# Block 1's attention: projections cut into pieces of six matmuls, one carried along by each step of the heads

## The chip, the core and the metric

One core of a Trainium2 chip runs one program: three transformer blocks in a row over 512 tokens of width 1024, in float32. The metric is the device time of one execution in microseconds (us). The matrix engine is TensorE (PE), with VectorE (DVE), ScalarE (ACT), GpSimd (POOL) beside it, and SyncE (SP), which issues most of the DMAs.

## The reference, cut to what matters

Only the mixer of the first block is touched by the change.

```python
h = rms_norm(x, mix_norm[l])
proj = h @ w_in[l]
qa, ka, va, qb, kb, vb = [proj[..., offs[i]:offs[i + 1]] for i in range(6)]
# 8 heads of two 32-wide halves, each with a relative bias
s1 = einsum(q1, k1) * scale + bias;  s2 = einsum(q2, k2) * scale + bias
p = softmax(s1) - lam * softmax(s2);  oa = p @ va
oa = rms_norm(oa, diff_subln[l]) * (1.0 - lambda_init)
# 8 heads of 64, four to each of two key/value heads
qb = rms_norm(qb, q_norm[l]); kb = rms_norm(kb, k_norm[l])
qb = apply_rope(qb, cos, sin); kb = apply_rope(kb, cos, sin)
ob = softmax(qb @ kb.T * scale) @ vb
x = x + concatenate([oa, ob], axis=-1) @ w_out[l]
```

## The kernel before

Activations lie transposed, as 8 panels of 128 features by 512 tokens. A float32 product is made of three fp32r matmuls, high by high, high by low and low by high (`mm3x`, lines 116 to 122). So a weight panel of 128x1024 goes through four stations: its load on SP's queue (`raw`, line 157), its high part on ACT and its low part on DVE, or on GpSimd where `pool_lo` is set (both in `weight`, lines 137 and 138), and 24 matmuls of 512 columns on PE.

`mix1` has two phases. In "att", `heads1` makes the projections and the heads, and `half_res` adds the first half of the output product (8 panels of 12 matmuls) to the residual. In "wo" the second half follows (line 526).

`heads1` first projects keys and queries: `rope(4)` for the rotated keys of the grouped heads, and for c = 0 and 1 `proj_q`, `proj_k` and `rope(c)`: 7 panels. A projected panel q or k is scaled on DVE (`scaled`, line 595), split into high and low part in a tile `hl` of which there is one (`HL = 1`; `parts`, lines 481 and 482), written to DRAM (line 487), and read back row by row as the operands of a head (`operand`, line 602; `keys`, line 586; `mk_gqa`, line 678). The panels of `rope` are normed over the head, rotated (GpSimd, lines 572 and 573) and take the same way. The values are projected by `v_tokens` with tokens as output rows, in two halves of 320 columns (192 matmuls).

`attend` runs 16 heads, a differential one and a grouped one by turns, in 4 steps of 128 queries, then 4 steps for the last head's values. A step makes the scores of this head (line 615 or 639, banks a and b), their softmax (DVE lines 617, 623, 624, 629, 640; ACT line 473; GpSimd lines 626 and 627 in steps 0 and 2), and one key chunk of the product with the values for the head before it (`values`): 4 transposes (line 450, banks c and d), a copy on ACT (line 458) and a subtraction on DVE (line 459), and two matmuls (lines 460 and 461), or one in plain float32 for the last chunk (line 454). The last matmul of a step is put down in `marks`.

The other projections hang on the heads: at a grouped head with r = 0, `mk_gqa` projects q and k for c + 2, for c = 0 `v_tokens` too, and `mk_diff` with r = 1 makes `rope(c + 2)`; all 24 matmuls of a panel stand in one block of the program, bank h. `half_res` comes after the heads in the program; each of its panels is told to go on PE after a mark of the second half of the heads (`M0`, `M1`), and its low parts are made by GpSimd (`PA`).

The order of the instructions on each engine is not written out: a list scheduler of the compiler takes, by modelled times, what is ready, earlier program text first. `issue_after(i)` adds that what it encloses comes after i on i's engine.

Of the kernel before, what the change touches and what calls it, by code (L numbers as in the profile page):

```python
# [33 lines left out]
class K:  # L34
# [3 lines left out]
    NL = 4  # L38
    AH = 2
    HL = 1  # L40
    PLH = 4
# [3 lines left out]
    PQ = (0, 2)  # L45
    M0 = 4
    M1 = 30
    PA = True
    OWN = 3
# [368 lines left out]

    def attend(self, heads):
# [72 lines left out]

    def v_tokens(self, src, xhl, vt, rtok, nh):

        nc = self.nc
        for half in range(2):
            pv = [self.psum("cdef") for _ in range(4)]
            for k0, kn in ((0, 3), (3, 3), (6, 2)):
                W = self.weight(src[half][:, k0 * 320:(k0 + kn) * 320], kn * 320, kn)
                for q in range(4):  # L500
                    s = slice(q * 128, (q + 1) * 128)
                    self.mm3x(pv[q][:, :320], [(xhl[k0 + k][0][:, s], xhl[k0 + k][1][:, s]) + W[k] for k in range(kn)], k0 == 0, k0 == 6)
            for q in range(4):
                hv = vt[q][:, half * 5:half * 5 + 5]
                pvv = pv[q][:, :320].rearrange("p (h d) -> p h d", h=5)
                nc.scalar.activation(hv[:, :, 0:64], pvv, AF.Copy, scale=rtok[:, q:q + 1])
                nc.vector.scalar_tensor_tensor(out=hv[:, :, 64:128], in0=pvv, scalar=rtok[:, q:q + 1], in1=f32v(hv[:, :, 0:64]), op0=ALU.mult, op1=ALU.subtract)

    def mix1(self, inp, gnext):
        nc, D = self.nc, self.D  # L510
        xhl, (rb, rtok), res = inp
        outer = self.ph
        gs = self.ph.tile([128, 1], F32, name="subln")
        nc.vector.tensor_scalar(out=gs, in0=self.vec("diff_subln"), scalar1=1.0 - (0.8 - 0.6 * math.exp(-0.0)), scalar2=None, op0=ALU.mult)
        gq, ind = self.vec("qk_norm1"), self.vec("ind1")
        ocs = [self.keep("oc", 8) for _ in range(8)]
        with self.phase("att"):
            self.heads1(xhl, rb, rtok, gq, ind, ocs)
            part = self.half_res(ocs, gs, res)
# [14 lines left out]

    def half_res(self, ocs, gs, res):

        nc, D = self.nc, self.D
        ohl = self.o_parts(ocs, gs, (0, 4, 1, 5), "x", 16)
        part = self.dr.tile([8, 128, 512], F32, name="part")
# [9 lines left out]
        return part  # L549

    def heads1(self, xhl, rb, rtok, gq, ind, ocs):
        nc, D = self.nc, self.D
# [3 lines left out]

        def rope(c, name, kind="pj"):

# [3 lines left out]
            f0 = self.t("rf0")  # L562
            nc.vector.tensor_mul(f0, self.proj(D["w1_in"][8 + c], xhl, kind=kind), rb)
            st = self.psum("st")
# [11 lines left out]
            nc.vector.scalar_tensor_tensor(out=f, in0=p, scalar=1.0 if c == 4 else -0.125, in1=rot, op0=ALU.mult, op1=ALU.mult)  # L576
            return self.parts(f, name)

        d = rope(4, "kpd", "mm")

        def keys(kv):
            ds = []
            for i in range(2):
                t = self.keep("kg", 2, F32R)
                for r in range(2):
                    nc.sync.dma_start(out=f32v(t[64 * r:64 * r + 64]), in_=self.part_rows(d, i, 32 * kv, [(64, 2), (1, 32)]))
                ds.append(t)
            return ds


        vt = [self.keep("vt", 4, F32R, w=1280).rearrange("p (h d) -> p h d", h=10) for _ in range(4)]

        def scaled(tag, p, scale):
            f = self.t("af")
            nc.vector.scalar_tensor_tensor(out=f, in0=p, scalar=scale, in1=rb, op0=ALU.mult, op1=ALU.mult)
            return self.parts(f, tag)

        def operand(tag, d, r, order):

            t = self.keep(tag, 3, F32R, tag="op1", w=1024).rearrange("p (r w) -> p r w", r=2)  # L600
            for b, o in enumerate(order):
                nc.sync.dma_start(out=f32v(t[32 * b:32 * b + 32]), in_=self.part_rows(d, o, 64 * r, [(1, 32), (32, 2)]))
            return t

        def diff_head(h, sms, q2, k2):
# [4 lines left out]
            def unit(q):  # L610
                mx = self.small("mx", 2, 4)
                es = []
                for s in range(2):
                    p = self.psum("scores")
                    nc.tensor.matmul(p, q2[:96, s, q * 128:(q + 1) * 128], k2[:96, s], start=True, stop=True)
                    e0 = self.ld("e0") if s == 0 else self.keep("e1", 12)
# [27 lines left out]

        qds, kds, qgd = {}, {}, {}

# [8 lines left out]

        def proj_q(c, kind="pj"):
            qds[c] = scaled("qdd", self.proj(D["w1_in"][c], xhl, kind=kind), -(32 ** -0.5))

        def proj_k(c, kind="pj"):
            kds[c] = scaled("kdd", self.proj(D["w1_in"][4 + c], xhl, kind=kind), 1.0)  # L660

        def mk_diff(c, r):
            if r == 1:
                qgd[c + self.AH] = rope(c + self.AH, "qpd") if c < 4 - self.AH else None
            return diff_head(2 * c + r, sms[c], operand("qd", qds[c], r, (0, 0, 1)), operand("kd", kds[c], r, (0, 1, 0)))

        def mk_gqa(c, r):
            if r == 0:
                if c == 0:
                    self.v_tokens(D["w1_v"], xhl, vt, rtok, 5)  # L670
                if c % 2 == 0:
                    kg[c // 2] = keys(c // 2)
                if c < 4 - self.AH:
                    proj_q(c + self.AH)
                    proj_k(c + self.AH)
            t = self.keep("qg", 2, F32R)
            for i in range(2):
                nc.sync.dma_start(out=f32v(t[64 * i:64 * i + 64]), in_=self.part_rows(qgd[c], i, 32 * r, [(64, 2), (1, 32)]))
            return gqa_head(r, sms[4 + c], t, kg[c // 2])

# [17 lines left out]

        for c in range(self.AH):
            proj_q(c, "mm")  # L700
            proj_k(c, "mm")
            qgd[c] = rope(c, "qpd", "mm")
        heads = []
        for c in range(4):
            for r in range(2):
                h = 2 * c + r
                heads.append((lazy(lambda c=c, r=r: mk_diff(c, r)), [v[:, h] for v in vt], r, ocs[c], normed(c) if r else None))
                heads.append((lazy(lambda c=c, r=r: mk_gqa(c, r)), [v[:, 8 + h // 4] for v in vt], r, ocs[4 + c], normed(4 + c) if r else None))
        self.attend(heads)

# [1260 lines left out]
def layout(I):  # L1971
# [8 lines left out]
    A["w1_in"] = panels(np.concatenate([w[:, :1024], w[:, 1536:2176][:, perm]], 1))  # L1980
    A["w1_v"] = moving(np.concatenate([w[:, 1024:1536], w[:, 2176:]], 1), 320)

# [71 lines left out]
```

## Time and profile before

| | us |
|---|---|
| median of three runs | 2684.18 |
| lowest to highest run | 2683.64 to 2689.05 |
| the profiled execution | 2690.05 |
| its span, from first to last instruction | 2688.2 |

The profile is of one execution, 5.9 us above the median. Its page gives the busy time of each engine over the span; views of the trace give the same for stretches, the chain of work that ended last, single instructions in order of time, and groups of instructions. A busy PE is not a PE at its rate: a matmul's shown duration includes its way through the array, and the next one starts before it ends. The rate is the distance between starts.

### The profile page before, as it was taken

The page shows a single profiled execution, that of the slowest core. Times are in us where ns is not written, and L with a number is a line of the kernel's source. Part 1 is how long each engine was busy: PE and PEld are TensorE (multiplying, and loading weights), DVE is VectorE, ACT ScalarE, POOL GpSimd, SP SyncE. Part 2 cuts the span into 40 slices and gives each one's busy share as a digit, 9 for nine tenths or more (in the row PEclk, how much of TensorE's full clock was granted, in tenths as well). Part 3 has the DMA queues.
Part 4 walks back from the last instruction along what each step waited for, and adds up shares of the span by engine and source line. Part 5 has one row for each costly group of instructions (what it writes and reads, how often), then busy time and mean ns, then how long its engine had stood idle before and what let it go on. Part 6 is the DMA issues. An engine that isn't in the chain of part 4 may idle for free.

```text
span 2688.2 us, 31177 instructions
## 1 busy us (share of the span) xinstructions
PE 2603.7 (97%) x11820; PEld 2104.6 (78%) x11820; DVE 1558.5 (58%) x2416; ACT 1057.1 (39%) x1622; POOL 410.6 (15%) x335
## 2 busy tenths in 40 slices
PE   8999998989999999999999899999899899999999
PEld 7887787767888887988788677888788777878787
DVE  7866555888544544567433654333545977747564
ACT  4222233666422324555323533223433454424242
POOL 1011012232000004133112301001210313101000
PEclk9999999989999999999999899999999999999999
DMA  5565644433522324422224342222524634223223
GB/s 197 179 202 196 202 154 140 141 99 123 193 94 94 94 93 148 133 100 71 94 96 140 110 144 91 97 98 95 179 73 148 208 99 148 100 94 97 94 92 110
DMA packets 114593, 340.00 MB, mean 126 GB/s; under 512 B 13784, under 2 KB 15768, under 8 KB 114314
## 3 DMA queue, kind: packets, MB, share of 16 engines
q1 hardware_dynamic: 104010, 301.02, 34.3%
q0 software_dynamic: 10432, 36.97, 4.4%
q8 instruction: 93, 1.52, 0.2%
q14 instruction: 58, 0.48, 0.1%
HBM read 301.47 MB, written 40.67 MB: 127 GB/s over the span
## 4 chain that ended last, share of the span: by engine, by line
PE 79%; issue 8%; DVE 5%; DMA 4%; ACT 2%; POOL 1%; SPq 0%; POOLq 0%; ACTq 0%; DVEq 0%
PE c L122 4%; PE a L120 4%; PE a L122 4%; PE c L120 4%; PE e L122 4%; PE a L121 4%; PE e L121 4%; PE c L121 4%; PE e L120 4%; PE b L122 4%; PE b L120 4%; PE b L121 4%; PE f L120 4%; PE d L120 4%; PE d L121 4%
## 5 line engine op out<-in xcount | busy, mean ns | idle before, releaser
L137 ACT ACTIVATE whi<-wraw 128x1024 fp32r<-128x1024 f32 (+5 forms) x422 | 426.0, 1012 | 1037.0 <-PE a L121 180.0
L138 DVE TENSOR_TENSOR wlo<-wraw,whi 128x1024 fp32r<-128x1024 f32 (+5 forms) x410 | 494.3, 1208 | 349.7 <-ACT whi L137 327.1
L120 PE MATMUL e<-xh,whi 128*128 128x512 f32 x368 | 145.1, 394 | 1.6 <-ACT xh L884 1.6
L121 PE MATMUL e<-xl,whi 128*128 128x512 f32 x368 | 145.8, 396 | 0.4 <-DVE xl L885 0.4
L122 PE MATMUL e<-xh,wlo 128*128 128x512 f32 x368 | 144.9, 394 | 0.8 <-DVE wlo L138 0.8
L121 PE MATMUL a<-xl,whi 128*128 128x512 f32 x352 | 139.0, 395 | 4.6 <-DVE xl L182 4.6
L120 PE MATMUL a<-xh,whi 128*128 128x512 f32 x352 | 139.5, 396 | 0.5 <-ACT whi L137 0.5
L122 PE MATMUL a<-xh,wlo 128*128 128x512 f32 x352 | 138.7, 394 | 0.9 <-DVE wlo L138 0.9
L120 PE MATMUL c<-xh,whi 128*128 128x512 f32 x352 | 138.7, 394 | 0.0
L121 PE MATMUL c<-xl,whi 128*128 128x512 f32 x352 | 138.7, 394 | 0.0
L122 PE MATMUL c<-xh,wlo 128*128 128x512 f32 x352 | 138.2, 393 | 0.0
L120 PE MATMUL b<-xh,whi 128*128 128x512 f32 x304 | 120.9, 398 | 10.1 <-ACT xh L181 7.6
L122 PE MATMUL b<-xh,wlo 128*128 128x512 f32 x304 | 120.4, 396 | 1.8 <-DVE wlo L138 1.8
L178 ACT ACTIVATE hh<-h 128x512 fp32r<-128x512 f32 x98 | 61.8, 631 | 148.5 <-DVE h L357 92.6
L121 PE MATMUL b<-xl,whi 128*128 128x512 f32 x304 | 120.2, 395 | 0.0
L896 POOL TENSOR_TENSOR acc<-sq 128x512 f32<-128x512 f32 x11 | 15.4, 1397 | 666.7 <-ACT sq L284 401.4
L122 PE MATMUL f<-xh,wlo 128*128 128x512 f32 x280 | 109.4, 391 | 0.6 <-DVE wlo L138 0.6
L120 PE MATMUL f<-xh,whi 128*128 128x512 f32 x280 | 109.8, 392 | 0.0
L121 PE MATMUL f<-xl,whi 128*128 128x512 f32 x280 | 109.5, 391 | 0.0
L122 PE MATMUL d<-xh,wlo 128*128 128x512 f32 x272 | 106.5, 392 | 0.0
L121 PE MATMUL d<-xl,whi 128*128 128x512 f32 x272 | 106.4, 391 | 0.0
L120 PE MATMUL d<-xh,whi 128*128 128x512 f32 x272 | 106.4, 391 | 0.0
(1144 smaller groups left out, 6427.6 us busy)
## 6 DMA issues: line engine op xcount, KB each, us to landing
wraw<-w_up SPq DMA_DIRECT2D x76, 512.0 KB
mw<-w_mod POOLq DMA_DIRECT2D x48, 512.0 KB, 4.6
wraw<-ffn_w_gate SPq DMA_DIRECT2D x43, 512.0 KB
wraw<-ffn_w_up SPq DMA_DIRECT2D x43, 512.0 KB
wraw<-w_down SPq DMA_DIRECT2D x40, 512.0 KB
wraw<-ffn_w_down SPq DMA_DIRECT2D x32, 448.0 KB
wraw<-w_gate SPq DMA_DIRECT2D x24, 512.0 KB
wraw<-ffn_w_down SPq DMA_DIRECT2D x16, 512.0 KB
```

Source lines behind the costliest of these rows:

```text
L120: mm(out, ah, bh, start=(first and i == 0), stop=False)
L121: mm(out, ah, bl, start=False, stop=False)
L122: self.last_mm = mm(out, al, bh, start=False, stop=(last and i == n - 1)).ins
L137: nc.scalar.activation(hi[:, i:j], raw[:, i:j], AF.Copy)
L138: (nc.gpsimd if self.pool_lo else nc.vector).tensor_sub(lo[:, i:j], raw[:, i:j], f32v(hi[:, i:j]))
L178: nc.scalar.activation(hi, x, AF.Copy)
L896: i = (self.nc.vector if c == 6 else self.nc.gpsimd).tensor_add(a, acc, s).ins
```

## The change

- `v_tokens` is gone. The values are projected like q and k, as 5 panels of 24 matmuls with features as output rows, scaled, and turned into token rows by 4 transposes of 128x128 a panel (`turn_v`); their weight is laid out in panels.
- Ahead of the heads stand 6 panels: q0, k0, rope(4), rope(0), and the values v0 and v4.
- The other 12 panels (q, k, rope, v for c = 1 to 3) and the 8 of `half_res` become a generator that yields after every 6 matmuls: 64 pieces, one in each of the 64 steps with scores. A piece goes on PE after the last matmul with values of its step (of its scores, in the first head).
- GpSimd makes the low parts of the weights of all 20 panels of the generator.
- A head's operands are loaded one head earlier (`ahead_diff`, `ahead_gqa`), with one more buffer for them, for the keys and for `hl`.
- The ring of four small names (`SECOND`) is taken from each phase's own pool.

```diff
-    AH = 2
-    HL = 1
+    HL = 2
@@ def t
-            return self.tp.tile([128, 512], dt, name=name, tag="v", bufs=3)
+            return self.ph.tile([128, 512], dt, name=name, tag="v", bufs=3)
@@ def attend(self, heads, fill=None)
                 if pv:
                     self.values(pv, q)
+                if fill and unit:
+                    with self.tc.issue_after(self.marks[-1] if pv else self.last_score):
+                        next(fill, None)
...
+        for _ in fill or ():
+            pass
@@
+    def proj_pieces(self, src, xhl, evac, kind="pj"):
+        W = self.weight(src, 1024, 8)
+        p = self.psum(kind)
+        for k in range(0, 8, 2):
+            self.mm3x(p, [W[k] + xhl[k], W[k + 1] + xhl[k + 1]], k == 0, k == 6)
+            if k == 6:
+                evac(p)
+            yield
@@ def half_res
-            self.pool_lo = self.PA
-            with self.tc.issue_after(self.marks[32 + self.M0 + self.M1 * c // 8]):
-                p = self.proj(D["w_out"][c][:, :512], ohl, 4, "pj")
-            self.pool_lo = False
-            nc.vector.tensor_add(x, p, x)
-            nc.sync.dma_start(out=part[c], in_=x)
+            W = self.weight(D["w_out"][c][:, :512], 512, 4)
+            p = self.psum("pj")
+            for k in range(0, 4, 2):
+                self.mm3x(p, [W[k] + ohl[k], W[k + 1] + ohl[k + 1]], k == 0, k == 2)
+                if k == 2:
+                    nc.vector.tensor_add(x, p, x)
+                    nc.sync.dma_start(out=part[c], in_=x)
+                yield
@@ def heads1
+        def turn_v(p, c):
+            f = self.t("vf")
+            nc.vector.tensor_mul(f, p, rb)
+            p = self.psum("st")
+            for q in range(4):
+                nc.tensor.transpose(p[:, q * 128:q * 128 + 128], f[:, q * 128:q * 128 + 128], self.ident)
+            p = p.rearrange("p (q h d) -> p q h d", q=4, h=2)
+            nc.scalar.activation(vt[c][:, :, :, 0:64], p, AF.Copy)
+            nc.vector.tensor_sub(vt[c][:, :, :, 64:128], p, f32v(vt[c][:, :, :, 0:64]))
...
+        def ahead_diff(c, r):
+            ops[c, r] = operand("qd", qds[c], r, (0, 0, 1)), operand("kd", kds[c], r, (0, 1, 0))
...
+        def mk_diff(c, r):
+            ahead_gqa(c, r)
+            return diff_head(2 * c + r, sms[c], *ops[c, r])
+
+        def mk_gqa(c, r):
+            if (c, r) != (3, 1):
+                ahead_diff(c + r, 1 - r)
+            return gqa_head(r, sms[4 + c], ops[4 + c, r], kg[c // 2])
...
+        for kind, c in (("q", 0), ("k", 0), ("g", 4), ("g", 0), ("v", 0), ("v", 4)):
+            src, evac = chunk(kind, c)
+            evac(self.proj(src, xhl))
+            if kind == "k":
+                ahead_diff(0, 0)
+
+        def fill():
+            self.pool_lo = True
+            for c in range(1, 4):
+                for kind in "qkgv":
+                    yield from self.proj_pieces(*chunk(kind, c)[:1], xhl, chunk(kind, c)[1])
+            yield from rest()
+            self.pool_lo = False
...
-        self.attend(heads)
+        self.attend(heads, fill())
```

## Rows read from the trace of the kernel before

**Rows 1.** The page, part 1: the span, and busy time of each engine.
```profile
span 2688.2 us, 31177 instructions
PE 2603.7 (97%) x11820; PEld 2104.6 (78%) x11820; DVE 1558.5 (58%) x2416; ACT 1057.1 (39%) x1622; POOL 410.6 (15%) x335
```

**Rows 2.** PE in order of time: start, duration, line, out<-in, idle time before.
```profile
385.07 0.39 PE L120 MATMUL a<-xh,whi 128*128 128x512 f32 x1
...
410.10 0.39 PE L120 MATMUL e<-xh,whi 128*128 128x512 f32 x1
...
415.55 0.39 PE L120 MATMUL f<-xh,whi 128*128 128x512 f32 x1
...
427.83 0.31 PE L120 MATMUL c<-whi,xh 128*128 128x320 f32 x1
...
430.03 0.31 PE L120 MATMUL d<-whi,xh 128*128 128x320 f32 x1
...
448.96 0.76 PE L615 MATMUL a<-kd,qd 96*128 96x512 f32 x1 [5.66 <-DMA qd<-qdd]
...
669.65 0.50 PE L120 MATMUL b<-oh,whi 128*128 128x512 f32 x1
```

**Rows 3.** Chain that ended last, 480 to 720 us: start, length, what.
```profile
506.09 0.79 PE g L208 x8
...
512.12 0.44 PE c L450 x4
512.56 0.86 PE f L454 x2
...
536.79 1.02 PE g L225 x16
...
564.58 11.28 DMA kg<-kpd
...
577.82 7.84 DMA kd<-kdd
```

**Rows 4.** Windows: stretch, length, PE, PEld, DVE, ACT, POOL busy, PEclk, DMA share, GB/s.
```profile
427.80:456.00 28.20, 19.55 (x104) 18.55 (x103) 11.91 (x24) 7.93 (x14) 5.31 (x6) 0.82 0.46 137
...
480.00:555.00 75.00, 69.80 (x366) 53.07 (x365) 60.12 (x138) 51.87 (x112) 24.20 (x17) 0.99 0.33 112
555.00:605.00 50.00, 41.85 (x193) 29.76 (x192) 43.88 (x120) 35.51 (x85) 16.99 (x14) 0.81 0.36 107
605.00:655.00 50.00, 48.94 (x266) 36.87 (x265) 43.66 (x105) 37.42 (x87) 19.02 (x14) 1.00 0.39 124
```

**Rows 5.** Chain that ended last, 395 to 480 us.
```profile
425.31 9.02 DMA qdd<-hl
...
436.47 8.51 DMA kdd<-hl
```

**Rows 6.** Windows of line 450 alone (transposes): stretch, length, PE busy (count).
```profile
480.00:555.00 75.00, 14.09 (x92) 0.99 0.33 112
555.00:605.00 50.00, 13.12 (x68) 0.81 0.36 107
605.00:655.00 50.00, 13.07 (x84) 1.00 0.39 124
```

**Rows 7.** Groups by line: form, count | busy us, mean ns | idle before, releaser.
```profile
L138 POOL TENSOR_TENSOR wlo<-wraw,whi 128x512 fp32r<-128x512 f32 x8 | 10.8, 1352 | 32.2 <-ACT whi L137 25.1 <-PE d L450 7.0
...
L595 DVE SCALAR_TENSOR_TENSOR af<-h,rb 128x512 f32<-128x512 f32 x4 | 2.7, 686 | 4.9 <-PE h L122 4.9
```

**Rows 8.** Windows of line 120 alone (a third of all projection matmuls).
```profile
480.00:555.00 75.00, 17.13 (x43) 0.99 0.33 112
```

**Rows 9.** GpSimd and VectorE in order of time.
```profile
427.99 1.31 POOL L573 TENSOR_TENSOR rot<-ra,rot 128x512 f32<-128x512 f32 x1
...
428.17 1.15 DVE L199 SCALAR_TENSOR_TENSOR ry<-ru,ry 128x8 f32<-128x8 f32 x1
...
429.75 0.17 DVE L199 SCALAR_TENSOR_TENSOR rr<-ru,ry 128x8 f32<-128x8 f32 x1
```

More of the change, by code (lines that the diff above doesn't have):

```diff
@@ L45 @@
     PQ = (0, 2)
-    M0 = 4
-    M1 = 30
-    PA = True
     OWN = 3
@@ L417, in proj, with attend @@
         return p
-    def attend(self, heads):
+    def attend(self, heads, fill=None):
         nc = self.nc
@@ L491, in part_rows @@
         return bass.AP(tensor=d.tensor, offset=d.offset + row * 1024 + part * 512, ap=[[s * 1024, n] for s, n in dims] + [[1, 512]])
[L493 to L507, printed above, removed]
+    def proj_pieces(self, src, xhl, evac, kind="pj"):
[6 more added lines that the diff above has]
+            yield
     def mix1(self, inp, gnext):
@@ L517, in mix1 @@
         with self.phase("att"):
-            self.heads1(xhl, rb, rtok, gq, ind, ocs)
-            part = self.half_res(ocs, gs, res)
+            part = self.dr.tile([8, 128, 512], F32, name="part")
+            self.heads1(xhl, rb, gq, ind, ocs, lambda: self.half_res(ocs, gs, res, part))
         with self.phase("wo"):
@@ L533, in o_parts, with half_res @@
         return [o[c] for c in sorted(cs)]
-    def half_res(self, ocs, gs, res):
+    def half_res(self, ocs, gs, res, part):
         nc, D = self.nc, self.D
         ohl = self.o_parts(ocs, gs, (0, 4, 1, 5), "x", 16)
-        part = self.dr.tile([8, 128, 512], F32, name="part")
         for c in range(8):
@@ L542, in half_res, with heads1 @@
             nc.sync.dma_start(out=x, in_=res[c])
-            self.pool_lo = self.PA
-            with self.tc.issue_after(self.marks[32 + self.M0 + self.M1 * c // 8]):
-                p = self.proj(D["w_out"][c][:, :512], ohl, 4, "pj")
-            self.pool_lo = False
-            nc.vector.tensor_add(x, p, x)
-            nc.sync.dma_start(out=part[c], in_=x)
-        return part
-    def heads1(self, xhl, rb, rtok, gq, ind, ocs):
+            W = self.weight(D["w_out"][c][:, :512], 512, 4)
[6 more added lines that the diff above has]
+                yield
+    def heads1(self, xhl, rb, gq, ind, ocs, rest):
         nc, D = self.nc, self.D
@@ L555, in heads1, with rope @@
         nc.sync.dma_start(out=cs, in_=D["rope1"])
-        def rope(c, name, kind="pj"):
+        def rope(p, c):
             i = int(c == 4)
             f0 = self.t("rf0")
-            nc.vector.tensor_mul(f0, self.proj(D["w1_in"][8 + c], xhl, kind=kind), rb)
+            nc.vector.tensor_mul(f0, p, rb)
             st = self.psum("st")
@@ L576, in rope @@
             nc.vector.scalar_tensor_tensor(out=f, in0=p, scalar=1.0 if c == 4 else -0.125, in1=rot, op0=ALU.mult, op1=ALU.mult)
-            return self.parts(f, name)
-        d = rope(4, "kpd", "mm")
+            gds[c] = self.parts(f, "kpd" if c == 4 else "qpd")
         def keys(kv):
@@ L583, in keys, with scaled @@
             for i in range(2):
-                t = self.keep("kg", 2, F32R)
+                t = self.keep("kg", 3, F32R)
                 for r in range(2):
-                    nc.sync.dma_start(out=f32v(t[64 * r:64 * r + 64]), in_=self.part_rows(d, i, 32 * kv, [(64, 2), (1, 32)]))
+                    nc.sync.dma_start(out=f32v(t[64 * r:64 * r + 64]), in_=self.part_rows(gds[4], i, 32 * kv, [(64, 2), (1, 32)]))
                 ds.append(t)
             return ds
-        vt = [self.keep("vt", 4, F32R, w=1280).rearrange("p (h d) -> p h d", h=10) for _ in range(4)]
-        def scaled(tag, p, scale):
+        vt = [self.keep("vt", 5, F32R, w=1024).rearrange("p (q h d) -> p q h d", q=4, h=2) for _ in range(5)]
+        def turn_v(p, c):
[7 more added lines that the diff above has]
+            nc.vector.tensor_sub(vt[c][:, :, :, 64:128], p, f32v(vt[c][:, :, :, 0:64]))
+        def scaled(ds, c, tag, p, scale):
             f = self.t("af")
             nc.vector.scalar_tensor_tensor(out=f, in0=p, scalar=scale, in1=rb, op0=ALU.mult, op1=ALU.mult)
-            return self.parts(f, tag)
+            ds[c] = self.parts(f, tag)
         def operand(tag, d, r, order):
-            t = self.keep(tag, 3, F32R, tag="op1", w=1024).rearrange("p (r w) -> p r w", r=2)
+            t = self.keep(tag, 4, F32R, tag="op1", w=1024).rearrange("p (r w) -> p r w", r=2)
             for b, o in enumerate(order):
@@ L614, in unit @@
                     p = self.psum("scores")
-                    nc.tensor.matmul(p, q2[:96, s, q * 128:(q + 1) * 128], k2[:96, s], start=True, stop=True)
+                    self.last_score = nc.tensor.matmul(p, q2[:96, s, q * 128:(q + 1) * 128], k2[:96, s], start=True, stop=True).ins
                     e0 = self.ld("e0") if s == 0 else self.keep("e1", 12)
@@ L643, in gqa_head @@
             return unit
-        qds, kds, qgd = {}, {}, {}
+        qds, kds, gds, ops = {}, {}, {}, {}
         def lazy(mk):
@@ L654, in lazy, with chunk, ahead_gqa @@
             return unit
[L656 to L675, printed above, removed]
+        def chunk(kind, c):
+            return {"q": (D["w1_in"][c], lambda p: scaled(qds, c, "qdd", p, -(32 ** -0.5))),
+                    "k": (D["w1_in"][4 + c], lambda p: scaled(kds, c, "kdd", p, 1.0)),
+                    "g": (D["w1_in"][8 + c], lambda p: rope(p, c)),
+                    "v": (D["w1_v"][c], lambda p: turn_v(p, c))}[kind]
+        def ahead_diff(c, r):
+            ops[c, r] = operand("qd", qds[c], r, (0, 0, 1)), operand("kd", kds[c], r, (0, 1, 0))
+        def ahead_gqa(c, r):
+            if r == 0 and c % 2 == 0:
+                kg[c // 2] = keys(c // 2)
             t = self.keep("qg", 2, F32R)
             for i in range(2):
-                nc.sync.dma_start(out=f32v(t[64 * i:64 * i + 64]), in_=self.part_rows(qgd[c], i, 32 * r, [(64, 2), (1, 32)]))
-            return gqa_head(r, sms[4 + c], t, kg[c // 2])
+                nc.sync.dma_start(out=f32v(t[64 * i:64 * i + 64]), in_=self.part_rows(gds[c], i, 32 * r, [(64, 2), (1, 32)]))
+            ops[4 + c, r] = t
+        def mk_diff(c, r):
[5 more added lines that the diff above has]
+            return gqa_head(r, sms[4 + c], ops[4 + c, r], kg[c // 2])
         kg = {}
@@ L697, in normed @@
             return done
[L699 to L702, printed above, removed]
+        for kind, c in (("q", 0), ("k", 0), ("g", 4), ("g", 0), ("v", 0), ("v", 4)):
[10 more added lines that the diff above has]
+            self.pool_lo = False
         heads = []
@@ L706, in heads1 @@
                 h = 2 * c + r
-                heads.append((lazy(lambda c=c, r=r: mk_diff(c, r)), [v[:, h] for v in vt], r, ocs[c], normed(c) if r else None))
-                heads.append((lazy(lambda c=c, r=r: mk_gqa(c, r)), [v[:, 8 + h // 4] for v in vt], r, ocs[4 + c], normed(4 + c) if r else None))
-        self.attend(heads)
+                heads.append((lazy(lambda c=c, r=r: mk_diff(c, r)), [vt[c][:, q, r] for q in range(4)], r, ocs[c], normed(c) if r else None))
+                heads.append((lazy(lambda c=c, r=r: mk_gqa(c, r)), [vt[4][:, q, h // 4] for q in range(4)], r, ocs[4 + c], normed(4 + c) if r else None))
+        self.attend(heads, fill())
     def tok_proj(self, src, lhs, nk, n, ntok, evac, kind="mm"):
@@ L1980, in layout @@
     A["w1_in"] = panels(np.concatenate([w[:, :1024], w[:, 1536:2176][:, perm]], 1))
-    A["w1_v"] = moving(np.concatenate([w[:, 1024:1536], w[:, 2176:]], 1), 320)
+    A["w1_v"] = panels(np.concatenate([w[:, 1024:1536], w[:, 2176:]], 1))
     A["w_out"] = panels(np.ascontiguousarray(I["w_out"][0].reshape(2, 2, 256, 1024).transpose(1, 0, 2, 3)).reshape(1024, 1024))
```

## Prediction

> **What bounds the kernel now.** The page first: PE is busy 97% of the span and no other engine over 58% [rows 1]. So a change that pays must take work from PE or close its gaps. This one takes no matmuls away; it moves them within one stage. I therefore bounded the stage with PE in order of time: the first projection matmul starts at 385.07, the first of the second half of `w_out` at 669.65 [rows 2]. The stage is 284.6 us long.
>
> Then what PE needs there at its rate. Busy time doesn't tell this; distances between starts do. 24 matmuls of 512 columns start within 5.45 us (410.10 to 415.55), 0.227 each; 15 of 320 columns within 2.20 (427.83 to 430.03), 0.147 each [rows 2]. A step's 4 transposes take 0.44, a plain float32 product, two records, 0.86, the 16 small ones of a norm 1.02, 8 for sums 0.79 [rows 3]. The sum:
> - attention: 224 matmuls (64 + 64 scores, 96 with values) x 0.227 = 50.8; 64 x 0.44 = 28.2; 16 x 0.86 = 13.8; 8 norms x 1.02 = 8.2; 4 x 0.79 = 3.2. Together 104.1, or 1.63 for each of the 64 steps.
> - 13 panels x 24 x 0.227 = 70.8; the values 192 x 0.147 = 28.2; `half_res` 96 x 0.227 = 21.8; five panels of `rope` x (0.79 + 0.44) = 6.2.
>
> That is 231.1, so PE loses 53.5 us in the stage. The windows tell where. From 427.8 to 456 PE's clock was granted at 0.82, part of it at the lower of its two levels, and PE started 104 matmuls, nearly all of the 0.147 kind, 15 of 28 us [rows 4]: about 13 are lost. The chain names the cause: the stores of q and k to DRAM, 9.02 and 8.51 us, one behind the other [rows 5], because there is one `hl`; the first scores end a wait of 5.66 for their operands [rows 2]. From 555 to 605, when the projections are used up, 68 transposes, 17 steps, took 50 us, 2.94 each where PE needs 1.63 [rows 6]; the clock was at 0.81 and PE busy for 41.85 [rows 4]; the chain there holds two waits for operands, 11.28 and 7.84 [rows 3].
>
> **The change part by part.** *Work of PE.* The values: 5 x 24 x 0.227 = 27.2 in place of 28.2, and 5 x 0.44 for turning = 2.2. So PE needs 1.2 us more, 232.3.
>
> *Ahead of the heads*: 6 panels, 32.7, two of them with `rope` and two with turning, 3.3: 36.0. q0 and k0 come first, each with an `hl` of its own, and four panels, 21.8 us, run while they are scaled, split (four passes of about 0.69 [rows 7]), stored (9.02 at worst) and read back. The read-back is bounded by the 5.66 that PE waited for it and by 11.28, the longest wait for an operand load [rows 2, 3]; I take the first, which is the same load: 0.69 x 4 + 9.0 + 5.7 = 17.5, under 21.8. With the far end it is 23, and PE waits 1 us. The rotated keys' and queries' way is longer, but the first differential head stands ahead of them. I book 2 us: 38 in all. If this cover fails the 13 us come back.
>
> *The steps.* PE needs 104.1 + 64 pieces x 6 x 0.227 (87.2) + three `rope` (3.7) + three turnings (1.3) = 196.3, 3.07 a step. What is lost on top must come from a stretch like it. The nearest is 480 to 555: 92 transposes are 23 steps [rows 6], and 3 x 43 = 129 projection matmuls [rows 8] are 5.6 a step. It needs 23 x 1.63 + 129 x 0.227 + 2.5 for two `rope` = 69.2 of 75 us: 5.8 lost, 0.25 a step. The bounds: 605 to 655, 21 steps in 2.38 each, with pieces as filler and nearly nothing lost [rows 6]; 555 to 605, 1.3 a step. I take 0.25, since that stretch has the same mixture: 64 x 3.32 = 212.3. Two heads differ: the first has no values beside it, the last one's values no pieces. I give their 8 steps what 555 to 605 lost, 1.3, so 8 x 1.05 = 8.4 more.
>
> *VectorE* must keep up. It was busy 60.12 in 23 steps, 43.88 in 17 and 43.66 in 21 [rows 4, 6], 2.1 to 2.6 a step. To this come the evacuations of 12 panels, partly in those numbers: by c two passes of 0.69 for q, k and v each, and some 3.8 for `rope`, 7.9 over 16 steps, 0.5. That is 2.6 to 3.1 against 3.32: covered, barely. The low parts leave it. Bank h is single: after each of the 20 panels the next piece waits for one pass of 0.69, with scores, transposes and values of a step between; the stretch taken has the same bank, so it is in the 0.25.
>
> *GpSimd*: 8 low parts of 512 columns took 1.352 each [rows 7], so one of 1024 is some 2.7, an estimate, one in four steps of 13 us. Two weight buffers let it start four steps ahead. Off the path, unless it holds VectorE (below).
>
> *Moved loads.* Each head's six loads (three for a grouped one's queries, four more for keys) now stand on SP's queue a head, some 13 us, earlier; a load that waits there for a store holds the weight loads behind it. A wait for a store was 9 at worst; three raw buffers are 12 steps of cover. That takes the 11.28 and 7.84 off the chain; what is late next is VectorE's part of the step. The small ring that moves between pools touches no line of this stage: booked at nothing.
>
> Sum: 38 + 212.3 + 8.4 = 258.7 against 284.6: 25.9 gained. On the profiled execution's 2690.05 that makes 2664; it lay 5.9 above the median, so against the median of 2684.18 it makes **2658**. With 0.15 to 0.4 a step it is 2648 to 2670.
>
> **The rivals.** *The pieces fill better.* If PE loses as little as from 605 to 655, 0.05 a step, 12.8 more come in: 2645. For it: there GpSimd made the low parts too. Against: its pieces were bound to an earlier mark and could wait until a hole came, while the new ones come ahead of the next step's transposes and cannot cover their own step's wait for the copy and the subtraction.
>
> *The start alone is gained.* The scheduler places the pieces so that the step's waits stay open, 0.5 a step: 16 us less, 2674. For it: the argument just given. Against: banks c and d let the next step's transposes run ahead.
>
> *Slower: GpSimd's low parts hold VectorE.* At 428.17 a VectorE pass of 128x8 with two inputs from SBUF took 1.15 and ended within 0.02 of GpSimd's pass that had begun at 427.99; the same line took 0.17 at 429.75 [rows 9]. So such a pass waits until GpSimd is done. If each 2.7 us low part holds VectorE for one and a half times its length, 4.05 in four steps, a step takes 2.58 + 0.5 + 1.0 = 4.08, not 3.32: 49 us, 2707. It decides from 3.72 a step (25.9 / 64 above 3.32), that is 2.6 us of holding for each panel, about one full low part. Against: VectorE spends most of a step on passes that read PSUM, and 605 to 655 shows no harm.
>
> The Trainium skill, GPSIMD Engine Reference, sections Specifications and Engine selection, speaks against the edit: GpSimd shares its SBUF interface with VectorE instructions that have two SBUF inputs, and two-input elementwise work belongs on VectorE, about twice as fast. The trace agrees on both (1.352 against some 0.69; the held pass); by that rule this last rival would be the forecast.
>
> **How the numbers follow.** Forecast 0.53, better filling 0.14, the start alone 0.17, slower 0.16. About 0.2%, 5.4 us, is what a measurement of this kernel can tell from no change, so faster means under 2678.8 and slower over 2689.5. Faster: 0.53 + 0.14 + 0.11 of the third = 0.78. Slower: 0.12 of the last, whose lighter cases (3.65 to 3.8 a step) give 0.04 and the third's bad end 0.06 to no change: 0.10. The range runs from a little under the best case, 2643, to 2690, where most of the last rival is left out.
>
> **What would show it.** In the profile after: the stage from the first projection to the second half of `w_out` near 259 us; first scores some 36 to 40 us after the first projection; no stretch with the clock near 0.8; steps of about 3.3 us, even from first to last; no operand load in the chain. Wrong: steps of 3.7 and more with VectorE busy throughout and its two-input passes ending with GpSimd's; or a chain that holds GpSimd's line 138, bank h's evacuation or operand loads; or other stages that move by more than 2 us.

## The result, and the profile after

The changed kernel takes 2706.14 us (median of 4 runs, 2703.87 to 2707.17) against 2683.91 for the kernel before: a ratio of 1.0079, 95% interval 1.0062 to 1.0097. It is slower, by 0.8%; the forecast was 2658, and 2690 was the far end of its range. The profiled execution took 2706.32.

The page of the changed kernel, part 1 (answering [rows 1]):

```profile
span 2704.6 us, 31071 instructions
PE 2609.9 (96%) x11768; PEld 2103.7 (78%) x11768; DVE 1554.6 (57%) x2405; ACT 1059.4 (39%) x1618; POOL 438.6 (16%) x347
```

PE in order of time in the changed kernel: the first projection, the first differential scores (line 619), the first grouped scores (line 643), the first matmul of the second half of `w_out` (answering [rows 2]; the columns are the same):

```profile
381.24 0.39 PE L116 MATMUL a<-xh,whi 128*128 128x512 f32 x1
...
417.62 0.39 PE L619 MATMUL a<-kd,qd 96*128 96x512 f32 x1
...
459.02 1.19 PE L643 MATMUL a<-kg,qg 128*128 128x512 f32 x2 [10.14 <-DMA qg<-qpd]
...
697.62 0.50 PE L116 MATMUL a<-oh,whi 128*128 128x512 f32 x1 [1.11 <-ACT oh L177]
```

The stage goes from 381.24 to 697.62: 316.4 us. It was 284.6 [rows 2] and was to be 258.7. The span grew by only 16.4, because the stage began 3.8 earlier than in before's profile and what follows it took 2007.0 instead of 2018.6. Within the stage the first 36.4 us are as forecast; then 41.4 pass until the first grouped scores, and 238.6 more until the end.

PE's waits from 381 to 698 in the changed kernel (engine, tile, line, what released it: us in total, times, the longest):

```profile
PE a L643 <- DMA qg<-qpd: 20.6, 4, 10.1
PE g L231 <- POOL hr L226: 5.3, 1, 5.3
PE a L619 <- DVE mx L621: 4.3, 4, 2.0
```

In four heads the grouped scores wait for their queries. The longest wait, followed back: GpSimd in order of time in the changed kernel, and then SP's queue (start, length of the issue, what):

```profile
431.91 2.49 POOL L134 TENSOR_TENSOR wlo<-wraw,whi 128x1024 fp32r<-128x1024 f32 x1
434.35 0.74 POOL L226 COPY hr<-rr 128x256 f32<-128x256 f32 x2
```

```profile
428.91 1.75 SPq L580 DMA_DIRECT2D kg<-kpd  x1
...
439.48 0.33 SPq L488 DMA_DIRECT2D qpd<-hl  x1
441.88 0.33 SPq L488 DMA_DIRECT2D qdd<-hl  x1
449.61 2.19 SPq L676 DMA_DIRECT2D qg<-qpd  x4
```

The row factors of the first rotated queries (`hr`) stand behind a low part. The queries are stored at 439.48; their loads can be issued only at 449.61, ten us later, and the scores start at 459.02, after nine more. What the DMA engines did meanwhile, in 40 slices from 439 to 460 us of the changed kernel (DMA: busy share of 16 engines in tenths):

```profile
DMA  8259911995111111111100010101013884111111
GB/s 281 66 238 406 375 47 55 411 410 202 55 47 47 55 55 55 47 55 55 47 31 16 12 31 23 55 31 43 23 51 133 300 261 117 20 43 51 51 51 51
```

Full stores run at some 400 GB/s with nine tenths of the engines busy. From 444 on long stretches run at about 50 GB/s with one tenth busy: these are the last loads of `kg`, then what is left of the two stores behind them, then, from 449.61 on, the loads of `qg`. The source of a load of `kg` or `qg` is two runs of 32 rows, `[(64, 2), (1, 32)]`; such loads are called narrow below. A load of 64 rows of 2 KB (131 KB) needs 2.6 us at 50 GB/s, and six of `kg` (issued from 426.33 on) and four of `qg` stand one behind the other.

What it costs PE, by windows of the changed kernel (stretch, length, PE, PEld, DVE, ACT, POOL busy, PEclk, DMA share, GB/s):

```profile
445.00:455.00 10.00, 3.88 (x17) 2.82 (x15) 0.00 (x0) 0.60 (x1) 0.00 (x0) 0.95 0.12 42
455.00:465.00 10.00, 5.98 (x14) 4.12 (x15) 1.49 (x3) 1.84 (x5) 0.00 (x0) 0.54 0.23 77
```

For ten us VectorE does nothing at all and PE has 17 matmuls; in the ten us after that the clock is granted at 0.54, nearly all at the lower of its two levels. So a wait costs something behind its end too: the two score matmuls at 459.02 took 1.19 us, and 0.62 in run 2, whose scores did not wait.

### The profile page after: what moved, and what is told of

It reads as the page before. It is cut to its first block, busy times and chain, and to the rows that moved or that the text cites. A ratio compares the mean times of both kernels' runs of the same rounds, so it can differ in the third digit from the quotient of the medians.

```text
span 2704.6 us, 31071 instructions
## 1 busy us (share of the span) xinstructions
PE 2609.9 (96%) x11768; PEld 2103.7 (78%) x11768; DVE 1554.6 (57%) x2405; ACT 1059.4 (39%) x1618; POOL 438.6 (16%) x347
## 5 line engine op out<-in xcount | busy, mean ns | idle before, releaser
L133 ACT ACTIVATE whi<-wraw 128x1024 fp32r<-128x1024 f32 (+3 forms) x421 | 426.2, 1015 | 1031.3 <-PE d L117 181.6
L134 DVE TENSOR_TENSOR wlo<-wraw,whi 128x1024 fp32r<-128x1024 f32 (+4 forms) x397 | 478.5, 1208 | 332.7 <-ACT whi L133 329.7
L116 PE MATMUL d<-xh,whi 128*128 128x512 f32 x360 | 141.4, 393 | 1.6 <-ACT xh L901 1.6
L117 PE MATMUL d<-xl,whi 128*128 128x512 f32 x360 | 141.3, 392 | 0.0
L118 PE MATMUL d<-xh,wlo 128*128 128x512 f32 x360 | 140.9, 391 | 0.0
L117 PE MATMUL a<-xl,whi 128*128 128x512 f32 x280 | 110.5, 395 | 4.4 <-DVE xl L178 4.4
L118 PE MATMUL e<-xh,wlo 128*128 128x512 f32 x288 | 112.8, 392 | 0.8 <-DVE wlo L134 0.8
L117 PE MATMUL e<-xl,whi 128*128 128x512 f32 x288 | 113.3, 393 | 0.0
L116 PE MATMUL e<-xh,whi 128*128 128x512 f32 x288 | 112.9, 392 | 0.0
L116 PE MATMUL a<-xh,whi 128*128 128x512 f32 x280 | 111.1, 397 | 0.0
```

Of the source, the lines that this page charges most:

```text
L116: mm(out, ah, bh, start=(first and i == 0), stop=False)
L117: mm(out, ah, bl, start=False, stop=False)
L118: self.last_mm = mm(out, al, bh, start=False, stop=(last and i == n - 1)).ins
L133: nc.scalar.activation(hi[:, i:j], raw[:, i:j], AF.Copy)
L134: (nc.gpsimd if self.pool_lo else nc.vector).tensor_sub(lo[:, i:j], raw[:, i:j], f32v(hi[:, i:j]))
```

## The experiments

Theory: the loads in two runs of rows cost the time. Rivals: the order of the panels (the rotated ones come too late for their heads), and GpSimd's low parts (the slower rival of the prediction). In the expectations of runs 1 to 4, D stands for the loads themselves, L for operands late by the order of the panels, G for GpSimd; in run 5's, L names the loads in two runs. Later runs ask what is left once the loads are mended. The stage is read from each kernel's own profile, from the first projection matmul to the first matmul of the second half of `w_out`, so it is of one execution each; 2 and 9, and 8 and 10, which differ by the edit of run 9 alone, lie within 0.1 us of each other in it. The ratio is to the kernel before on the same chip.

| kernel | median us | ratio, 95% interval | stage us |
|---|---|---|---|
| before | 2683.91 | | 284.6 |
| changed | 2706.14 | 1.0079 [1.0062, 1.0097] | 316.4 |
| 1 rotated panels first | 2743.77 | 1.0224 [1.0207, 1.0242] | 345.3 |
| 2 loads cut | 2681.49 | 0.9986 [0.9975, 0.9998] | 286.5 |
| 3 low parts on VectorE | 2705.80 | 1.0084 [1.0064, 1.0103] | 309.0 |
| 4 rotated first, loads cut | 2702.92 | 1.0075 [1.0056, 1.0094] | 299.7 |
| 5 before, loads cut | 2685.91 | 0.9998 [0.9986, 1.0011] | 281.3 |
| 6 before, two `hl` | 2696.99 | 1.0045 [1.0027, 1.0064] | 293.2 |
| 7 cut, one panel into the first head | 2683.04 | 0.9994 [0.9983, 1.0004] | 282.2 |
| 8 cut, pieces untied | 2677.24 | 0.9967 [0.9956, 0.9979] | 275.5 |
| 9 cut, first panel's low parts on VectorE | 2681.18 | 0.9977 [0.9967, 0.9987] | 286.4 |
| 10 as 8 and 9 | 2674.54 | 0.9955 [0.9938, 0.9972] | 275.6 |
| 11 cut, all low parts on VectorE | 2679.93 | 0.9975 [0.9966, 0.9985] | 283.9 |
| 12 cut, row factors on VectorE | 2675.49 | 0.9957 [0.9940, 0.9974] | 277.7 |
| 13 as 10 and 12 | 2677.40 | 0.9967 [0.9955, 0.9979] | 271.9 |

What follows the stage took between 2007 and 2024 us in these profiles, though no edit touches it. That part is not explained here (see the end of the next section), so questions about the stage are answered from the stage.

**1. The order.** The rotated panels first, both ahead of the heads and among the pieces:

```diff
-        for kind, c in (("q", 0), ("k", 0), ("g", 4), ("g", 0), ("v", 0), ("v", 4)):
+        for kind, c in (("g", 4), ("g", 0), ("q", 0), ("k", 0), ("v", 0), ("v", 4)):
...
-                for kind in "qkgv":
+                for kind in "gqkv":
```

> The changed kernel, with the rotated panels drawn forward: ahead of the heads rope(4) and rope(0) come first, then q0, k0, v0, v4; in the pieces the order for each c is rope, q, k, v. Theory L (the grouped heads' queries come too late: norm, rotation, store, load, one after the other): the first grouped scores start some 15 us sooner, the three later waits of 3.2 to 3.7 us for the queries and the half-clock stretches behind them go; 25 us less, about 2681. Theory G (GpSimd's low parts hold VectorE): no change, about 2706. Against both: q0 and k0 are now late, and the first scores wait some 5 us.

A miss by both. PE's waits in this kernel, 386 to 732:

```profile
PE a L619 <- DMA kd<-kdd: 30.5, 1, 30.5
PE a L619 <- DMA qd<-qdd: 20.1, 3, 9.3
```

No grouped head waits for queries any more; the differential heads wait instead, and longer. Whichever panel comes last has its store and its loads behind the narrow ones. With narrow loads the order decides who waits, not whether.

**2. The loads cut.** Each load of `kg` and `qg` in loads of 32 rows, twice as many (the edit for `qg`; that for `kg` is alike):

```diff
-            for i in range(2):
-                nc.sync.dma_start(out=f32v(t[64 * i:64 * i + 64]), in_=self.part_rows(gds[c], i, 32 * r, [(64, 2), (1, 32)]))
+            for i in range(4):
+                nc.sync.dma_start(out=f32v(t[32 * i:32 * i + 32]), in_=self.part_rows(gds[c], i // 2, 32 * r + 64 * (i % 2), [(1, 32)]))
```

> The changed kernel, but each load of 64 rows of the grouped heads' keys and queries, 2 groups of 32 rows, is cut into two loads of 32 rows. Theory D (a load of that shape runs on two of the sixteen DMA engines, some 24 packets of 2 KB a us, so that loads and the stores behind them take 8 to 13 us): the query loads land in 3 to 4 us, the store of the first queries in 3 instead of 10; the first grouped scores start some 12 us sooner and the later waits go; 20 us less, about 2686. If only the length of the chain ahead of the store counts (theory L alone): 5 us or less, about 2702. Theory G: 2706.

The theory holds: 24.7 us less than the changed kernel, 29.9 in the stage. SP's queue, then the DMA engines from 439 to 460 us, of the kernel with cut loads:

```profile
441.64 0.34 SPq L488 DMA_DIRECT2D qpd<-hl  x1
...
444.45 4.01 SPq L676 DMA_DIRECT2D qg<-qpd  x8
```

```profile
DMA  1000004990089974845469820000000000000000
GB/s 47 0 0 0 0 0 179 398 406 16 0 359 398 273 219 133 187 133 172 125 137 324 215 70 23 12 0 0 0 0 0 0 0 16 0 0 0 0 0 0
```

The loads of the queries can be issued 2.8 us after their store instead of 10.1, they run at some 125 to 190 GB/s (the 324 is with the next head's `qd` loads), and no grouped head waits for a DMA. PE in order of time, cut loads:

```profile
383.12 0.39 PE L116 MATMUL a<-xh,whi 128*128 128x512 f32 x1
...
419.51 0.39 PE L619 MATMUL a<-kd,qd 96*128 96x512 f32 x1
...
437.31 1.11 PE L231 MATMUL g<-ident,hr 128*128 128x128 f32 x4 [4.98 <-POOL hr L226]
...
451.95 0.62 PE L643 MATMUL a<-kg,qg 128*128 128x512 f32 x2
...
669.58 0.50 PE L116 MATMUL a<-oh,whi 128*128 128x512 f32 x1 [1.11 <-ACT oh L177]
```

But the stage, 286.5, is still no shorter than before's. The loads explain the loss, not the missing gain.

**3. GpSimd.** All low parts on VectorE, the loads as they were:

```diff
-            self.pool_lo = True
+            self.pool_lo = False
```

> The changed kernel with the low parts of all weights made by VectorE. Theory G, the rival of the prediction: GpSimd holds VectorE by 43 us or more in the stage; without it 15 to 20 us less, about 2688. Theories L and D: the passes of VectorE with two inputs from SBUF lost only some 18 us in the stage to anything at all, before 23, so nothing is gained; 12 panels of 1.2 us and 8 of 0.7 come onto VectorE, and it is the same or up to 8 us slower, 2706 to 2714.

The rival falls: 2705.80 against 2706.14. The stage is 7.4 shorter (309.0), with a wait for the row factors of 3.1 us in place of 5.3, but what follows it was longer in this profile (2012.4 against 2007.0), and theory G wanted 15 to 20 us less in time. PE's largest wait in this kernel's stage is still that for the queries:

```profile
PE a L643 <- DMA qg<-qpd: 21.0, 4, 15.1
```

**4. The edits of runs 1 and 2 together.**

> Both edits, rotated panels first and loads of 32 rows. Theories L and D together: no wait for queries is left, the steps take 3.3 to 3.5 us, the stage some 265 us; 2665 to 2675, under the kernel before (2684). If the steps themselves are slow (the pieces don't cover the waits of their step), it stays near 2690 or above.

A miss: 2702.92. With the rotated panels first, q0 and k0 have only two panels behind them to cover their way through DRAM, and PE's waits (386 to 687) show it:

```profile
PE a L619 <- DMA kd<-kdd: 12.7, 3, 9.7
```

The order q0, k0 first, which the prediction relied on, was right.

**5. The kernel before with cut loads** (the same edit there).

> The kernel before with only its qg and kg loads cut into loads of 32 rows. Theory L (the two-run loads cost wherever they are, and before's 11.28 us for the rotated keys is theirs): that wait falls to about 3 us and the stretch at half clock behind it shrinks, 2672 to 2676 us. Rival (the order of before, two pairs of panels ahead, hides the loads except their latency, and only the new order meets them): no change, 2683 to 2686 us. If before gains about as much as the changed kernel did (25 us), the reordering itself is worth nothing at all; if it gains nothing, the reordering is worth the 2 to 3 us that lie between before and the changed kernel with cut loads.

No change in time (0.9998), 3.3 in the stage. PE, first projection, first scores and second half of `w_out`, then a piece of the chain that ended last:

```profile
386.28 0.39 PE L120 MATMUL a<-xh,whi 128*128 128x512 f32 x1
...
442.39 0.48 PE L615 MATMUL a<-kd,qd 96*128 96x512 f32 x1
...
667.62 0.51 PE L120 MATMUL b<-oh,whi 128*128 128x512 f32 x1
```

```profile
433.07 4.54 DMA kdd<-hl
```

The same loads cost the kernel before nothing in time. That its rotated panels were made two pairs of panels ahead of the heads is the likely reason; no run shows it. They did hold up its front: the first scores come 56.1 us after the first projection (442.39 - 386.28) instead of 63.9, and the store of k takes 4.54 instead of 8.51 [rows 5], with one `hl` as before. But 4.5 of these 7.8 us are lost again behind it. The 11.28 and 7.84 of its chain [rows 3] are gone from this kernel's, and from 555 to 605 its clock is still granted at 0.80: they were not worth what they looked. The loss in time by narrow loads comes with the new order, and the reordering without them (run 2 against run 5) is worth, in time, some 3 to 4 us, and the two intervals overlap. It isn't gained in the stage, which is 5.2 longer (286.5 against 281.3), but behind it (2009.0 against 2018.9).

**6. The kernel before with two `hl`.**

```diff
-    HL = 1
+    HL = 2
```

> The kernel before with only two buffers for the split panels instead of one. The prediction held that before's front waited for that one buffer (stores of 9.02 and 8.51 us) and booked some 13 us there. If the buffer is the cause: 2670 to 2676 us, and the two stores leave the chain. Rival (the single buffer is not late, the queue behind the loads is): 2682 to 2686 us.

A miss, and on the other side: 0.45% slower. Its chain, 385 to 500 us:

```profile
425.58 8.81 DMA kdd<-hl
...
435.29 8.79 DMA kd<-kdd
444.27 0.77 PE b L615
```

The store no longer waits for the other one, yet takes 8.81, and the load behind it 8.79. The first scores come 59.6 us after the first projection (444.27 - 384.64) instead of 63.9: the one buffer was worth 4 us, not 13. Cutting the loads of the rotated keys, which stand ahead of these stores, was worth 7.8 (run 5). The stage came out 8.6 longer, lost later, where this run does not tell why.

**7. One panel into the first head.** With cut loads, v4 is no longer done ahead but as two pieces a step in the first head:

```diff
-        for kind, c in (..., ("g", 0), ("v", 0), ("v", 4)):
+        for kind, c in (..., ("g", 0), ("v", 0)):
...
+            yield from self.proj_pieces(*chunk("v", 4)[:1], xhl, chunk("v", 4)[1])
...
-                        next(fill, None)
+                        for _ in range(1 if pv else 2):
+                            next(fill, None)
```

> The changed kernel with cut loads, and the last panel ahead of the heads (the shared values, 24 of 5.45 us / 24 matmuls) taken instead as two pieces a step in the first head, where TensorE lost 13 of 20 us. Theory F (the first head lacks work to fill it): about 5 us less than with the cut loads alone, 2675 to 2677 us, with 0 to 7 lost in the first head. Rival H (the first head waits for its own chain: VectorE's passes and the rotated queries behind GpSimd's queue): no gain, 2680 to 2684 us.

Split: the stage is 4.3 shorter, as theory F had it, but the time is not (the stretch behind the stage took 2019.1 against 2009.0).

**8. Pieces untied.** With cut loads, without the tie to the step's last values matmul:

```diff
-                    with self.tc.issue_after(self.marks[-1] if pv else self.last_score):
-                        next(fill, None)
+                    next(fill, None)
```

> The changed kernel with cut loads, its pieces no longer tied to the step's last values matmul (the planner puts them where it likes). Theory T (the tie itself makes the 0.5 us a step that is lost beyond the need, since a piece may not start before the values are done): steps of 3.3 us, 2670 to 2675 us. Rival (the tie keeps the pieces spread evenly; without it they run ahead and the later heads are bare): slower than with the cut loads, 2690 us or more.

PE, first projection and second half of `w_out`:

```profile
384.04 0.39 PE L116 MATMUL a<-xh,whi 128*128 128x512 f32 x1
...
659.50 0.50 PE L116 MATMUL a<-oh,whi 128*128 128x512 f32 x1
```

The stage is 11.0 shorter, the time 4 to 5 us (the intervals of runs 2 and 8 just overlap). The first head, from its first scores to the first grouped ones, takes 28.7 instead of 32.4, and what follows 210.4 instead of 217.6, 0.12 us a step. So the tie does cost, but 0.1 us a step, not the 0.3 that theory T wanted. (The expectations of runs 10 and 13 take 280 us for this stage: that counts to the second group of matmuls of the second half, at 664.25, and not to its first matmul.)

**9 to 11. Low parts once more, with cut loads.** First (run 9) the low parts of the first piecewise panel alone; run 11 is the edit of run 3, run 10 the edits of runs 8 and 9:

```diff
-            self.pool_lo = True
             for c in range(1, 4):
                 for kind in "qkgv":
+                    self.pool_lo = (kind, c) != ("q", 1)
```

> The changed kernel with cut loads, and only the first panel that is taken along in pieces makes its low parts on VectorE; all later ones on GpSimd as in the change. Theory P (the first head's loss comes from GpSimd's queue: the row factors of the first rotated queries, 5.0 us late, stand behind that panel's low parts and the first head's weights): that wait falls under 2 us, the first head loses some 8 instead of 13.5 us, stage 280 to 283 us (286.5 with cut loads alone), time 2674 to 2678 us. Rival V (VectorE, busy 21.1 of the 25.2 us, takes the extra 1.2 us passes ahead of the head's own): stage 286 to 290 us, 2681 to 2686 us.

Nothing moved in the stage (286.4). GpSimd in order of time in this kernel says why:

```profile
433.13 2.55 POOL L134 TENSOR_TENSOR wlo<-wraw,whi 128x1024 fp32r<-128x1024 f32 x1
435.63 0.74 POOL L226 COPY hr<-rr 128x256 f32<-128x256 f32 x2
```

The row factors of the first rotated queries still stand behind a low part: it is the third panel's, not the first's. I had taken the wrong panel.

> The changed kernel with cut loads and all low parts on VectorE, so that the prediction's slower rival (GpSimd's low parts hold VectorE) is asked again where no narrow load covers it. Theory G (GpSimd holds VectorE by 0.76 us or more a step): some 40 us less in the stage, 2640 us. Theory P (only the first head's queue on GpSimd counts): as with the first panel alone, 2674 to 2680 us. Rival V (VectorE's own time counts): 2684 to 2690 us.

With all low parts on VectorE the wait for the row factors fell from 5.0 to 3.1 and the stage by 2.6 to 283.9. The copy of the row factors now stands behind a pass of the first head's weights on GpSimd (2.63 us from 429.14). Neither the 40 us of theory G nor the loss of theory V came.

> Cut loads, untied pieces and the first panel's low parts on VectorE together. If the gains add (untied took 6 us out of the stage, theory P 4 to 6): stage 274 to 277 us, 2670 to 2674 us. If both fill the same gap: as untied alone, stage 280 us, 2677 us.

The stage, 275.6, is that of run 8: nothing added, as run 9 lets one expect. The time, 2674.54, is the lowest of the study; its interval overlaps those of runs 8 and 12.

**12. The row factors on VectorE.** With cut loads, only the two small copies of a rotated panel moved:

```diff
-                nc.gpsimd.tensor_copy(e[:, :, i * 64:i * 64 + 64]...
+                nc.vector.tensor_copy(e[:, :, i * 64:i * 64 + 64]...
```

> The changed kernel with cut loads, and the copy that spreads the row factors of rotated panels made by VectorE instead of GpSimd (two copies a panel). In the first head it stood behind a GpSimd low part of 2.34 us and the head's weights while VectorE had nothing to do from 433.5 to 437.7. Theory P (GpSimd's queue in the first head): the 5.0 us wait of the turning matmuls goes to 1 or less, with the half clock behind it shorter: stage 279 to 283 us against 286.5, time 2674 to 2678 us. Rival (something else ends at the same time, the head's own weights or the values' transposes): stage 285 to 288 us, 2680 to 2684 us.

PE in order of time in this kernel, then GpSimd and VectorE:

```profile
382.11 0.39 PE L116 MATMUL a<-xh,whi 128*128 128x512 f32 x1
...
431.88 1.08 PE L231 MATMUL g<-ident,hr 128*128 128x128 f32 x4 [3.68 <-DVE rs L628]
...
659.76 0.51 PE L116 MATMUL a<-oh,whi 128*128 128x512 f32 x1 [1.11 <-ACT oh L177]
```

```profile
429.18 2.40 POOL L134 TENSOR_TENSOR wlo<-wraw,whi 128x1024 fp32r<-128x1024 f32 x1 [1.30 <-ACT whi L133]
429.12 2.61 DVE L226 COPY hr<-rr 128x256 f32<-128x256 f32 x2
```

The stage is 8.8 shorter, 277.7, better than expected, though the wait fell only to 3.7: the turning matmuls ran at 431.88, 49.8 after the first projection, where with cut loads they ran at 54.2. Of the 8.8, 4.8 are in the first head (27.6 from its first scores to the first grouped ones, against 32.4). What cost was mainly the place of these copies in GpSimd's queue, behind low parts and the head's weights. But holding shows as well, and is the likely reason why the wait fell no further: the two moved copies took 2.61 us here, until GpSimd's low part was over, where such a pair took 0.49 at 410.13.

**13. The edits of runs 8, 9 and 12 together,** on the cut loads.

> Cut loads, untied pieces, the first panel's low parts and the row factors' copies on VectorE. If theory P holds beside the untied pieces: the first head's waits for GpSimd (2.0 us for the row factors there) go, stage 276 to 279 us, 2670 to 2673 us. If they were covered: 280 us and 2674 us, as without the copies moved.

The stage, 271.9, is the shortest, 3.6 under run 8 and 5.8 under run 12. Alone their edits took 11.0 and 8.8 off run 2's, together 14.6, so the gains overlap in part. The time, 2677.40, is no better: what follows the stage took 2024.2 in this profile, the most of all.

## Why the prediction was wrong

**What PE needs, and the front: right.** The first scores were to come 36 to 40 us after the first projection; they came at 36.4 in the changed kernel. Four panels behind q0 and k0 do cover their way. The reason given for before's loss there, "because there is one `hl`", was mostly wrong: a second `hl` was worth 4 us of the 13 (run 6), and cutting the narrow loads ahead of the stores 7.8, with one `hl` (run 5).

**The step that failed first: "the rotated keys' and queries' way is longer, but the first differential head stands ahead of them. I book 2 us", and with it "a wait for a store was 9 at worst".** I put no figures on that way. In the changed kernel it is: the row factors at 434.35 to 435.14 (behind a low part on GpSimd), rotation and split until the store at 439.48, 10.1 for the store, 9.4 for the loads. The head ahead of it is over by 445, and VectorE empties. Three later heads lose 3 to 4 us in the same place. Cutting the loads takes 29.9 us out of the stage, 9.0 of it before the first grouped scores (417.62 to 459.02 against 419.51 to 451.95) and 21.0 after. I had looked at the latencies of stores and loads (9.02, 8.51, 11.28, 7.84), taken them as constants, and not asked why 128 to 512 KB took as long as they did.

The row of the DMA engines shows the loads at about 50 GB/s with one tenth of 16 engines busy. The Trainium skill, DMA: Bandwidth & Descriptors, section "Why a DMA increments its semaphore by 16 and not by 1", states that a DMA is spread over the largest number of engines, up to 16, that divides the slowest dimension above one of both its patterns: two for `[(64, 2), (1, 32)]`, sixteen for 32 rows. The trace agrees: 47 to 55 GB/s and a share of 0.12, two in sixteen, against some 125 to 190 GB/s when cut.

**The second: "I take 0.25 [a step], since that stretch has the same mixture".** With cut loads the stretch from the first scores to the end is 250.1 us; I had 220.7. In the first head 32.4 pass until the grouped scores, where I had four steps and half of the 8.4, 17.5: 15 short. Behind it 217.6 against 203.2: 14.4 in 60 steps, 0.24 a step. So a step loses about 0.5, the figure of the rival "the start alone is gained"; a stretch where before still ran whole panels beside the heads was not like steps with one piece each. Run 8 gives back 11.0 by untying the pieces, which bears out the argument that this rival rested on, and run 12 gives back 8.8 by getting the row factors off GpSimd's queue. Both together (run 13) leave 271.9, 13.2 above the forecast: 7.2 in the first head (24.7 against 17.5), 7.6 behind it (210.8 against 203.2), less 1.6 ahead of it. PE's largest waits there are for the row factors (5.0 us in three) and for VectorE's part of the values (`ptl`, 4.8 in six); no run here parts that rest further. A slip in the sum: with 0.15 to 0.4 a step it gives 2652 to 2668, not 2648 to 2670.

**The moved loads, "that takes the 11.28 and 7.84 off the chain": worth little.** Cut loads in the kernel before took both out of its chain, 3.3 us out of its stage and nothing out of its time (run 5). A long piece in the chain of waits is not what one gains by removing it.

**The slower rival: not what came, though its 2707 lies beside the measured 2706 by luck.** Its mechanism, GpSimd's low parts holding VectorE, would have shown as steps of 4 us with VectorE busy throughout. VectorE was empty in the decisive stretch, and moving the low parts to it changed nothing in time and took 7.4 us off the stage (run 3), or 2.6 with cut loads (run 11), where the rival put 49 on the stage. Holding does occur: in the changed kernel three of VectorE's five passes at line 564, each beside a low part of GpSimd, took 2.36 to 2.55 us instead of 0.74, and run 12 shows it on the path. But by the count in run 3's expectation the passes with two inputs from SBUF lost some 18 us in the stage in all, against 23 in the kernel before: it did not grow. The rule quoted from the Trainium skill, GPSIMD Engine Reference, Engine selection, that such work belongs on VectorE, is worth no more here than these 2.6 to 7.4 us of the stage. What the prediction named as a sign against itself, a chain that holds operand loads, is what came.

**The other stages moved by more than 2 us,** which it had also named: the stretch behind the stage was 11.6 shorter than in before's profile, and between 2007 and 2024 over all kernels. The change shifts rings of buffers that later stages share, which may be the cause; no kernel was made to try that, and it stays open. It is large enough to hide or to feign half a per cent.

A version that beats both kernels: cut loads with the row factors on VectorE, 2675.49, 0.43% under the kernel before (interval 0.26 to 0.60), or run 10 at 0.45%.

## What to carry to other kernels

Before moving a load nearer to its use, compare its bandwidth with the fastest transfer in the same profile: a load far below it is narrow. Cutting it so that its outermost dimension is long cost little here: eight loads took 4.01 us of SP's queue where four took 2.19, and the kernel before was no slower for it (run 5). When a step of a plan says that something "stands ahead" of a long way, write that way out piece by piece with a number for each, queues of every engine included, as for the part one worries about. And take the loss of a step from a stretch with the same filler, not from the nearest one with the same engines.

## What the runs showed of the hardware

A narrow load holds back wide transfers behind it: what waits for the 512 KB store of the rotated queries could be issued 10.1 us after it with such loads in front and 2.8 when they were cut. An idle stretch costs something behind its end too: in the changed kernel 3.88 us of PE's work in ten were followed by ten at a granted clock of 0.54, the lower level for nearly all of it, just when the heads had their operands again. And a plain copy on VectorE can be held by GpSimd: the pair of run 12 took 2.61 us and ended within 0.2 of GpSimd's low part, where such a pair takes 0.49 undisturbed (410.13, same run).
